# Gates first beside the state space, then values and conv gates by seven products on a normalised x, and the convolution's output projection by seven products through memory

## The chip, the cores and the metric

The kernel runs on one core of one Trainium2 chip. The metric is the device time of one execution in microseconds (us). A core has TensorE (PE, with its weight loads PEld), VectorE (DVE), ScalarE (ACT), GpSimd (POOL) and SyncE (SP), each with an instruction queue that runs in order, and DMA engines that move data between memory and the on-chip buffers.

## What is computed

A decoder block on x of 1024 positions by 1024 channels, in float32:

```
proj = rmsnorm(x) @ w_in + b_in      # 512 + 5 * 1024 columns
u, bg, cg, val, gs, gc = split(proj)
y = s5(u)                            # diagonal state space, 32 groups of 16 channels, 64 complex states
z = gelu(y)
y_a = (z @ w_glu_a) * sigmoid(z @ w_glu_b)
y_b = (bg * causal_conv3(cg * val)) @ w_conv_out
merged = sigmoid(gs) * y_a + sigmoid(gc) * y_b
h = x + merged @ w_out
h = h + relu(rmsnorm(h) @ w_ff1) ** 2 @ w_ff2      # 4096 columns
out = rmsnorm(h)
```

## The kernel before

All data lie with channels on the 128 partitions and positions along the row. A float32 operand is cut into a high part of a reduced type and the rest, so each product of a 128x128 weight block with 512 positions takes three matmuls: high by high, high by low and low by high (`products`, L135 to L137). The weights come as 1024x128 blocks of 512 KB: `w_load` (L87) loads one on SyncE's queue, `w_split` makes its high part wh on ScalarE (L95) and the rest wl on VectorE (L96).

The program is written out in one order, and each engine runs its rows of it in that order. Phase 0 normalises x and makes the first three blocks of u beside it. Then the loop over `order` runs 57 jobs: one block of u, eight each of val, cg, bg, gs and gc (48 matmuls each), the convolution's output (co, eight jobs of 48), and the eight of glu. Here the input projection uses x before its normalisation and multiplies each result by rstd on VectorE when it leaves PSUM. Behind it come the output projection (pw, `wo_half`), the second norm, four blocks of FF1 in plain form (pp), and then FF1 and FF2 in groups of seven products: `seven` computes a 2 by 2 block matrix product with seven half-size products instead of eight (84 matmuls for 96). In it P1 to P7 take operands B11, t1, B21, n2, B22, t3, t4 of the one side and sums of weight blocks (gs, cut into gh and gl) of the other. Its results c11, c12, c22, c21 are taken out of PSUM by `done`. The FF1 results go to memory and come back as the operands of FF2.

Beside the matmuls runs the state space. `ssm_params` computes its parameters on POOL; `cut_u` copies u into the layout U, 16 small pieces for each of four tiles, half on ScalarE and half on VectorE; `ssm_step` runs eight steps. Each makes the kernels Bk and Vk on POOL (`outer`) and the phases cs and sn, then transposes and small products on TensorE (pst, psk), psx, a rotation and scans on VectorE (xr, xi), the rotation back (yr, t) and psy; odd steps end with a gelu. These are generators. After each fourth group of three matmuls, `draw` gives them credit by the matmul time and the factor `BESIDE` of the current job, and an instruction sequence is put there. A negative yield postpones by modelled TensorE time, a positive one costs credit. `drain` runs all that is left at once; it stands before job gs 1. `ssm_z` then turns U into z.

In groups and rows below, a number behind a name is a buffer or job. The stages of the profiled execution by TensorE: phase 0 to 44.26 us, input projection with convolution output to 641.40, glu to 728.4, output projection to 816.9, plain FF1 to 862.9, groups to 1415, the last slab to the end.

## Time and profile before

| what | value |
|---|---|
| time, median of 3 runs | 1479.4 us (1478.95 to 1479.52) |
| the profiled execution | 1478.85 us, its span 1477.1 |
| TensorE busy | 1445.2 us, 98% |
| weight loads, VectorE | 1198.2 us, 967.4 us |
| ScalarE, POOL | 552.1 us, 223.6 us |
| moved | 161.10 MB, 109 GB/s in the mean |

The span is the time from the first to the last instruction of the profiled execution; its own time is somewhat longer. Busy times overlap between engines. TensorE's rows are pipelined, so one matmul's duration is longer than the distance between two starts, and the latter is its price.

### The profile page before, as it was taken

What the parts mean: (1) busy time and instruction counts of PE and PEld (TensorE: products, weight loads), DVE (VectorE), ACT (ScalarE), POOL (GpSimd) and SP (SyncE); (2) the same over time, 40 slices, a digit from 0 to 9 for tenths busy, and PEclk for the clock granted to TensorE, in tenths of its full rate; (3) what the DMA queues carried; (4) which work ended last, traced back from release to release, by engine and by line L of the source; (5) the groups of instructions that cost most, each with busy time, mean ns of one, the idle gap of its engine ahead of it and who ended that gap; (6) DMA issues with size and microseconds to landing.
All of it is one profiled execution on the core that took longest, in us unless ns stands there. A gap on an engine that the chain in (4) does not pass through costs nothing.

```text
span 1477.1 us, 17137 instructions
## 1 busy us (share of the span) xinstructions
PE 1445.2 (98%) x6563; PEld 1198.2 (81%) x6563; DVE 967.4 (65%) x1445; ACT 552.1 (37%) x803; POOL 223.6 (15%) x474
## 2 busy tenths in 40 slices
PE   9969999999999999999999999999999999999997
PEld 7858888888888888888888888888887878787897
DVE  6667468768767545446625887777775266758575
ACT  6541423132132227423313444334433443424354
POOL 5891220120120000000010012222222010000000
PEclk9989999999999999999999999999999999999998
DMA  5011101111111011114311234555559468445302
GB/s 216 29 43 41 46 29 55 33 42 58 35 37 57 29 58 43 57 43 163 139 54 58 86 129 160 180 175 180 183 199 347 163 163 253 178 153 218 115 29 86
DMA packets 48961, 161.10 MB, mean 109 GB/s; under 512 B 6256, under 2 KB 10736, under 8 KB 48880
## 3 DMA queue, kind: packets, MB, share of 16 engines
q1 hardware_dynamic: 35888, 117.02, 23.2%
q0 software_dynamic: 12992, 43.00, 8.6%
q8 instruction: 51, 0.84, 0.2%
q14 instruction: 30, 0.25, 0.1%
HBM read 117.00 MB, written 42.99 MB: 108 GB/s over the span
## 4 chain that ended last, share of the span: by engine, by line
PE 88%; POOL 5%; DVE 3%; issue 1%; DMA 1%; ACT 1%; SPq 0%; DVEq 0%; ACTq 0%; POOLq 0%
PE ps L135 9%; PE ps L137 9%; PE ps L136 9%; PE seed L1093 5%; PE seed L1095 5%; PE seed L1094 5%; PE pa L1095 3%; PE pa L1094 3%; PE pa L1093 3%; PE pe L1093 3%; PE pe L1095 3%; PE pe L1094 3%; PE pc L135 2%; PE pc L137 2%; PE pg L136 2%; PE pg L135 2%
## 5 line engine op out<-in xcount | busy, mean ns | idle before, releaser
L135 PE MATMUL ps<-xh,wh 128*128 128x512 f32 x656 | 258.9, 395 | 1.2 <-ACT wh L95 1.2
L137 PE MATMUL ps<-xh,wl 128*128 128x512 f32 x656 | 256.2, 391 | 0.5 <-DVE wl L96 0.5
L136 PE MATMUL ps<-xl,wh 128*128 128x512 f32 x656 | 255.7, 390 | 0.0
L135 PEld LDWEIGHTS ps<-xh,wh 128*128 128x128 f32 x656 | 123.5, 188 | 28.3 <-ACT wh L95 1.6
L137 PEld LDWEIGHTS ps<-xh,wl 128*128 128x128 f32 x656 | 123.4, 188 | 27.4 <-DVE wl L96 1.4
L136 PEld LDWEIGHTS ps<-xl,wh 128*128 128x128 f32 x656 | 123.6, 188 | 25.3
L96 DVE TENSOR_TENSOR wl<-wr,wh 128x1024 fp32r<-128x1024 f32 x57 | 70.1, 1230 | 58.2 <-ACT wh L95 58.0
L95 ACT ACTIVATE wh<-wr 128x1024 fp32r<-128x1024 f32 x57 | 59.6, 1047 | 55.4 <-PE pc L136 24.0
L1065 DVE TENSOR_TENSOR gl<-gs,gh 128x1024 fp32r<-128x1024 f32 x52 | 63.4, 1219 | 6.4 <-ACT gh L1061 6.4
L898 POOL DMA_DIRECT2D hd<-h x16 | 9.0, 561 | 384.1 <-ACT ssum L900 309.0
L1061 ACT ACTIVATE gh<-gs 128x1024 fp32r<-128x1024 f32 x52 | 54.8, 1054 | 20.1 <-DVE gs L1057 14.7
L135 PE MATMUL pc<-vh,wh 128*128 128x512 f32 x128 | 51.0, 399 | 0.0
L1065 DVE TENSOR_TENSOR gl<-rg,gh 128x1024 fp32r<-128x1024 f32 (+1 forms) x52 | 48.4, 951 | 3.4 <-ACT gh L1061 2.7
L137 PE MATMUL pc<-vh,wl 128*128 128x512 f32 x128 | 49.9, 390 | 0.0
L135 PE MATMUL pw<-mh,hwo 128*128 128x512 f32 x128 | 49.9, 390 | 0.0
L137 PE MATMUL pw<-mh,lwo 128*128 128x512 f32 x128 | 49.8, 389 | 0.0
L136 PE MATMUL pc<-vl,wh 128*128 128x512 f32 x128 | 49.8, 389 | 0.0
L136 PE MATMUL pw<-ml,hwo 128*128 128x512 f32 x128 | 49.8, 389 | 0.0
L135 PE MATMUL pg<-zh,wh 128*128 128x512 f32 x128 | 49.8, 389 | 0.0
L136 PE MATMUL pg<-zl,wh 128*128 128x512 f32 x128 | 49.8, 389 | 0.0
L137 PE MATMUL pg<-zh,wl 128*128 128x512 f32 x128 | 49.8, 389 | 0.0
L861 DVE TENSOR_TENSOR g<-ps,rstd 128x512 f32<-128x512 f32 x32 | 21.7, 687 | 41.5 <-PE ps L137 41.4
(531 smaller groups left out, 3603.2 us busy)
## 6 DMA issues: line engine op xcount, KB each, us to landing
rg<-in_w SPq DMA_DIRECT2D x52, 512.0 KB, 4.5
wr<-in_win SPq DMA_DIRECT2D x41, 512.0 KB, 3.5
wr<-in_wco SPq DMA_DIRECT2D x8, 512.0 KB, 3.4
wr<-in_wglu SPq DMA_DIRECT2D x8, 512.0 KB, 3.4
rwo<-in_wo SPq DMA_DIRECT2D x8, 512.0 KB, 6.7
h<-in_x_t SPq DMA_DIRECT2D x8, 512.0 KB, 7.4
hd<-h POOLq DMA_DIRECT2D x16, 256.0 KB, 2.3
rw<-in_w SPq DMA_DIRECT2D x8, 512.0 KB, 6.9
```

Source lines behind the costliest of these rows:

```text
L95: A.activation(hi, r, AF.Copy)
L96: V.tensor_sub(lo, r, hi.bitcast(F32))
L135: T.matmul(ps, wh[:, j, :], xh[:, cols], start=start and i == 0, stop=False)
L136: T.matmul(ps, wh[:, j, :], xl[:, cols], start=False, stop=False)
L137: T.matmul(ps, wl[:, j, :], xh[:, cols], start=False, stop=stop and i == n - 1)
L861: V.tensor_mul(t, ps[hh], rstd[:, HS[hh]])
L898: nc.gpsimd.dma_start(hd[i][:, c], h[i][:, c])
L1061: A.activation(hi[nm], src[nm], AF.Copy)
L1065: V.tensor_sub(lo[nm], src[nm], hi[nm].bitcast(F32))
L1093: T.matmul(p, wh[:, kb, :], xh, start=first and kb == 0, stop=False, skip_group_check=True)
L1094: T.matmul(p, wh[:, kb, :], xl, start=False, stop=False, skip_group_check=True)
L1095: T.matmul(p, wl[:, kb, :], xh, start=False, stop=kb == 3, skip_group_check=True)
```

## The change

The jobs of the loop are now u 3, seven gs, seven gc and eight bg: 23 blocks of 48 matmuls, beside which the state space runs. Their results are put through their sigmoid and go to memory (gd) on ScalarE's queue. Blocks 0 and 1 still use the unnormalised operand. While they run, x is read again, scaled by rstd on VectorE, written to memory (xnd) and cut into the operands xw of all later blocks (`normed_in`); the last blocks also make the sums t1, n2, t3, t4 of them (`sums_of`). `drain` stands before the last block. Then 13 groups of seven products run: four pairs of a val and a cg group, one of gs 7 with gc 7, and four of the convolution's output. The gated convolution of a pair is computed on VectorE and ScalarE in steps between the products (`conv_step`), its parts and sums go to memory (xcd) by POOL's queue and come back as operands xc by SyncE's (`XC_LOADS`). The output groups multiply by the gates read back as yb and write yd; glu reads gs, yd and z (zd) from memory. In the state space, half of the rotation back (t2, t3) moves from VectorE to POOL, and the waits in modelled time are changed. `seven` and `group_steps` serve all groups by one list, with the seeds made before the first.

```diff
-PREPARE = 20.0
+PREPARE = 38.0
...
-BESIDE = {"u": 0.4, "val": 0.62, "cg": 0.25, "bg": 0.38, "co": 0.28, "gs": 0.5, "gc": 0.5, "glu": 0.3}
+BESIDE = {"u": 0.4, "gs": 0.8, "gc": 0.8, "bg": 0.8}
...
-    order = [("u", 3)]
+    order = [("u", 3)] + [("gs", i) for i in range(7)] + [("gc", i) for i in range(7)] + [("bg", i) for i in range(8)]
...
-        yield 0.1
+        yield -3.0
...
-        yr, t2 = sh(f"yr{s}"), sh(f"t2{s}")
+        yr, t2, t3 = sh(f"yr{s}"), sh(f"t2{s}"), sh(f"t3{s}")
+        G.tensor_tensor(t2, xr, sn, op=ALU.mult)
+        G.tensor_tensor(t3, xi, cs, op=ALU.mult)
+        G.tensor_tensor(t3, t3, t2, op=ALU.add)
-        V.tensor_mul(t2, xr, sn)
-        V.tensor_mul(t, xi, cs)
-        V.tensor_add(t, t, t2)
-        yield 1.9
-        yield -4.0
+        yield -6.0
...
+            for q in range(4):
+                for j in range(CH):
+                    o, i = zv[32 * q:32 * q + 32, j, :], U[b][32 * j:32 * j + 32, q, :]
+                    if (q + j) % 2:
+                        A.activation(o, i, AF.Copy, scale=0.5)
+                    else:
+                        V.tensor_scalar(o, i, 0.5, None, op0=ALU.mult)
+                yield 0.8
+            nc.scalar.dma_start(zd[b], zt)
...
+    def split_out(nm, dst, t, lo=None):
+        hi = half(f"h{nm}", F32R)
+        A.activation(hi, t, AF.Copy)
+        nc.gpsimd.dma_start(dst("h"), hi.bitcast(F32))
+        def rest():
+            V.tensor_sub((t if lo is None else lo).bitcast(F32R), t, hi.bitcast(F32))
+            nc.gpsimd.dma_start(dst("l"), t if lo is None else lo)
+        later.append(rest)
...
+    def gated_conv(i):
+        v = val[i]
+        g = late.tile([P, S], F32, tag="l", name=f"bgt{i}")
+        nc.sync.dma_start(g, gd["bg", i])
+        o = og[i] = unit(f"og{i}")
+        A.activation(o, v, AF.Identity, scale=col(C_CW + 16 + i), bias=col(C_CB + i))
+        yield
+        for back in (1, 2):
+            V.scalar_tensor_tensor(
+                o[:, back:], v[:, :S - back], col(C_CW + 16 - 8 * back + i), o[:, back:], op0=ALU.mult, op1=ALU.add
+            )
+        yield
+        V.tensor_mul(o, o, g)
+    def to_xc(m, name, t, lo=None):
+        split_out(f"xc{name}{m}", lambda part: xcd[name, part][:, m, :], t, lo)
...
+    def conv_first(m):
+        yield from gated_conv(m)
+        f11, f12 = (og[m][:, c] for c in HS)
+        ta = og["a", m] = unit(f"xca{m}")
+        t1 = ta[:, HS[0]]
+        V.tensor_sub(t1, f11, f12)
+        to_xc(m, "B11", f11, half(f"lf11_{m}"))
+        to_xc(m, "t1", t1)
+        yield
+    def conv_second(m):
+        yield from gated_conv(m + 4)
+        (f11, f12), (f21, f22) = ([og[i][:, c] for c in HS] for i in (m, m + 4))
+        t3 = og["a", m][:, HS[1]]
+        n2, t4 = (unit(f"xcb{m}")[:, c] for c in HS)
+        V.tensor_sub(t3, f12, f22)
+        V.tensor_sub(n2, f11, t3)
+        yield
+        V.tensor_sub(t4, f21, n2)
+        to_xc(m, "B21", f21)
+        yield
+        to_xc(m, "n2", n2)
+        to_xc(m, "B22", f22)
+        yield
+        to_xc(m, "t3", t3)
+        to_xc(m, "t4", t4)
+        yield
...
+    def done_cg(m, quad, ps, less):
+        r, c = row_of(quad)
+        i = m + 4 * r
+        y, b = val[i][:, c], col(C_BIN + base["cg"] + i)
+        if less is not None:
+            t = half(f"cg{quad}_{m}")
+            V.tensor_sub(t, ps, less)
+            ps = t
+        V.scalar_tensor_tensor(y, ps, b, y, op0=ALU.add, op1=ALU.mult)
+        if quad == "c12":
+            conv.append(conv_first(m))
+        elif quad == "c21":
+            conv.append(conv_second(m))
...
+    def gate_load(g):
+        for o in (2 * g, 2 * g + 1):
+            yb[o] = unit(f"yb{o}")
+            nc.sync.dma_start(yb[o], gd["gc", o])
...
+    def done_co(g, quad, ps, less):
+        r, c = row_of(quad)
+        y = yb[2 * g + r]
+        if less is not None:
+            t = half(f"co{quad}_{g}")
+            V.tensor_sub(t, ps, less)
+            ps = t
+        V.tensor_mul(y[:, c], ps, y[:, c])
+        if quad in ("c21", "c12"):
+            nc.gpsimd.dma_start(yd[2 * g + r], y)
...
+    for m in range(4):
+        for k, f in (("val", done_val), ("cg", done_cg)):
+            add_group(from_rows(win[base[k] + m], win[base[k] + m + 4]), of_w, partial(f, m))
+    add_group(from_rows(win[base["gs"] + 7], win[base["gc"] + 7]), of_w, done_gate)
+    first_co = len(groups)
+    for g in range(4):
+        add_group(from_wco(2 * g, 2 * g + 1), of_c, partial(done_co, g))
+    first_f1 = len(groups)
+    for g in range(N_GROUP):
...
+    def normed_in(k, hh):
+        c = HS[hh]
+        t = half(f"xn{k}_{hh}")
+        nc.sync.dma_start(t, x_t[k * P:(k + 1) * P, c])
+        V.scalar_tensor_tensor(t, t, col(C_G1 + k), rstd[:, c], op0=ALU.mult, op1=ALU.mult)
+        nc.scalar.dma_start(xnd[k][:, c], t)
+        put(xw, f"B{1 + k // 4}{1 + hh}", k % 4, t)
...
+    def sums_of(kb):
+        (b11, b12), (b21, b22) = ([xn_raw[k][:, c] for c in HS] for k in (kb, kb + 4))
+        t = half(f"xt1_{kb}")
+        V.tensor_sub(t, b11, b12)
+        put(xw, "t1", kb, t)
+        V.tensor_sub(b12, b12, b22)
+        V.tensor_sub(b11, b11, b12)
+        put(xw, "n2", kb, b11)
+        put(xw, "t3", kb, b12)
+        V.tensor_sub(b21, b21, b11)
+        put(xw, "t4", kb, b21)
...
+    for n in range(n_main):
+        k, i = order[n]
+        clock["job"] = k
+        w_load(n + 2)
+        w_split(n + 1)
+        w_load(n + 3)
+        last = n == n_main - 1
+        ps = [bank(f"ps{n}_{j}") for j in range(2)]
+        if n < 2:
+            wh, wl = parts[n]
+            for kb, (xh, xl) in enumerate(xg):
+                for hh, c in enumerate(HS):
+                    T.matmul(ps[hh], wh[:, kb, :], xh[:, c], start=kb == 0, stop=False)
+                    T.matmul(ps[hh], wh[:, kb, :], xl[:, c], start=False, stop=False)
+                    T.matmul(ps[hh], wl[:, kb, :], xh[:, c], start=False, stop=kb == 7)
+            for kb in range(4 * n, 4 * n + 4):
+                for hh in range(2):
+                    normed_in(kb, hh)
+            if n == 1:
+                lows()
+        else:
+            if last:
+                group_load(0)
+                drain()
+                cvs.close()
+                late = ctx.enter_context(tc.tile_pool(name="late", bufs=12))
+            if n >= n_main - 3:
+                sums_of(n - (n_main - 3))
+            for hh in range(2):
+                xs = [operand(xw, f"B{1 + kb // 4}{1 + hh}", kb % 4) for kb in range(8)]
+                products(ps[hh], parts[n], range(8), xs, slice(0, HALF))
+        if n >= n_main - 4:
+            sums_load(n - (n_main - 4))
+        if k == "u":
+            evac_u(i, ps)
+            start(cut_u())
+            start(ssm_step(0))
+            continue
+        for hh in range(2):
+            t = half(f"e{n}_{hh}")
+            src = ps[hh]
+            if n == 1:
+                V.tensor_mul(t, src, rstd[:, HS[hh]])
+                src = t
+            A.activation(t, src, AF.Identity if k == "bg" else AF.Sigmoid, bias=col(C_BIN + base[k] + i))
+            nc.scalar.dma_start(gd[k, i][:, HS[hh]], t)
+    prep = group_steps(0, 0)
+    for _ in prep:
+        pass
...
+    XC_LOADS = {
+        0: [("B11", 0)], 1: [("B11", 1)], 2: [("t1", 0), ("t1", 1)], 3: [("B21", 0)], 4: [("n2", 0)],
+        5: [("B22", 0), ("B21", 1)], 6: [("t3", 0), ("n2", 1), ("B22", 1)], 7: [("t3", 1)], 8: [("t4", 0), ("t4", 1)],
+    }
...
+    for n in range(first_f1):
+        preps = [group_steps(n, 1), group_steps(n + 1, 0) if n + 1 < first_f1 else iter(())]
+        def after(i):
+            for prep in preps:
+                next(prep, None)
+            for _ in range(2 if n == first_co - 1 and i in (1, 2) else 1):
+                conv_step()
+            step_on()
+            for name, u in XC_LOADS.get(7 * (n - first_co + 1) + i, []):
+                xc_load(name, u)
+            if n >= first_co and i == 1:
+                gate_load(n - first_co)
+            if i == 6 and n + 2 < first_f1:
+                group_load(n + 2)
+            if n == first_f1 - 1:
+                if i == 2:
+                    glu_w[0] = raw_load(wglu[0], "glu0")
+                elif i == 4:
+                    glu_w[0] = cut(glu_w[0], "glu0", wtile)
+                if i in (3, 4, 5, 6):
+                    z_load(i - 3)
+                if i == 6:
+                    z_cut(0)
```

**TensorE, the end of the state space.** In before, psx of the last step and its psy have two blocks of the projection between them (ps is a block's PSUM, U the state space's input, yr and t the rotated states, ps_0_3872 to ps_1_3951 the two blocks):

```order
L539 MATMUL psxr_3841<-U_833,WT 128x256
L539 MATMUL psxi_3842<-U_833,WT 128x256
L135 MATMUL ps_0_3872<-xh_133,wh_3766 128x512
...
L137 MATMUL ps_1_3951<-xh_184,wl_3867 128x512
L573 MATMUL psy_4000<-U_833,Mk_204 128x256
L575 MATMUL psy_4000<-yr_3914,Vk_202 128x255
L575 MATMUL psy_4000<-t_3849,Vk_202 128x255
```

In the changed kernel the same place stands between block 21 (ps_1_2948) and block 22 (ps_0_3048); psy_3058 is of step 6, pst_3072, psxr_3087 and psy_3115 of step 7:

```order
L137 MATMUL ps_1_2948<-xhwB_934,wl_2804 128x512
L555 MATMUL psy_3058<-U_1067,Mk_203 128x256
...
L506 MATMUL pst_3072<-ident,Bk 128x128 x4
L509 MATMUL psk_3073<-Vk_202,Bk 32x128
L509 MATMUL psk_3073<-Vk_202,Bk 32x128 x3
L522 MATMUL psxr_3087<-U_1067,WT 128x256
...
L555 MATMUL psy_3115<-U_1067,Mk_204 128x256
L557 MATMUL psy_3115<-yr_3106,Vk_202 128x255
L557 MATMUL psy_3115<-t_3108,Vk_202 128x255
...
L135 MATMUL ps_0_3048<-xhwB_785,wh_2943 128x512
```

What moved: the 96 matmuls between psx and psy of the last step are gone, and its psy stands ahead of the last block.

**ScalarE, behind the first blocks.** In before, the cut of u (U) stands between two weight splits; v_1_0_839 is a result of the val block:

```order
L95 ACTIVATE wh_726<-wr_607 128x1024
L246 ACTIVATE U_746<-ut_609,pt 32x256 x8
L246 ACTIVATE U_763<-ut_612,pt 32x256 x8
L246 ACTIVATE U_804<-ut_615,pt 32x256 x8
L246 ACTIVATE U_833<-ut_723,pt 32x256 x2
L819 ACTIVATE v_1_0_839<-v_1_0_838,pt 128x512
L819 ACTIVATE v_1_1_843<-v_1_1_842,pt 128x512
L95 ACTIVATE wh_846<-wr_671 128x1024
```

In the changed kernel e is the gate of block 1 (e_1_956) and of block 2 (e_0_1076, e_1_1079), wh_960 the weights of block 3 and wh_1082 of block 4:

```order
L1136 DMA gsd_675<-e_1_956 128x512
L95 ACTIVATE wh_960<-wr_729 128x1024
L229 ACTIVATE U_980<-ut_609,pt 32x256 x8
L229 ACTIVATE U_1009<-ut_612,pt 32x256 x8
L229 ACTIVATE U_1038<-ut_615,pt 32x256 x8
L229 ACTIVATE U_1067<-ut_835,pt 32x256 x4
L1135 ACTIVATE e_0_1076<-ps_0_966,pt 128x512
L1136 DMA gsd_676<-e_0_1076 128x512
L1135 ACTIVATE e_1_1079<-ps_1_967,pt 128x512
L1136 DMA gsd_676<-e_1_1079 128x512
L95 ACTIVATE wh_1082<-wr_842 128x1024
```

What moved: the cut of u now stands two blocks later in the program, and two gates with their transfers stand between it and the next split.

**SyncE and VectorE, where the output groups begin.** Rows of SyncE in the changed kernel (xc are the operands of the convolution's output, rg weights of an output group, yb the gates gc that multiply the first output group's results); before has no such rows:

```order
L1154 DMA xlct_4677<-xct3l 128x1024
L1154 DMA xhct_4696<-xct4h 128x1024
L1154 DMA xlct_4698<-xct4l 128x1024
L1154 DMA xhct_4700<-xct4h 128x1024
L1154 DMA xlct_4702<-xct4l 128x1024
L1025 DMA yb_4704<-gcd_683 128x1024
L1025 DMA yb_4706<-gcd_684 128x1024
```

VectorE's rows at the same place (gs_10 and gl_10 belong to the weights of the second output group, gl_9 to the first's):

```order
L846 TENSOR_TENSOR gs_10_4724<-gs_10_4724,rg_0_4645 128x512
L1034 TENSOR_TENSOR yb_4704<-pa_4655,yb_4704 128x512
L857 TENSOR_TENSOR gl_9_4742<-rg_1_4421,gh_9_4722 128x512
L857 TENSOR_TENSOR gl_10_4744<-rg_0_4645,gh_10_4727 128x1024
L857 TENSOR_TENSOR gl_10_4761<-gs_10_4724,gh_10_4746 128x1024
```

What is new: yb stands behind all reads of xc on SyncE, and on VectorE two groups' weight splits stand behind the multiplication that needs it.

## Rows read from the trace of the kernel before

**Rows 1.** The page: GB/s moved in each of 40 equal slices of the span.

```profile
GB/s 216 29 43 41 46 29 55 33 42 58 35 37 57 29 58 43 57 43 163 139 54 58 86 129 160 180 175 180 183 199 347 163 163 253 178 153 218 115 29 86
```

**Rows 2.** Stretches: length, busy PE, PEld, DVE, ACT, POOL; granted clock, DMA share, GB/s.

```profile
44.26:641.40 597.14, 585.63 (x2609) 482.62 (x2608) 386.32 (x611) 205.03 (x292) 109.98 (x261) 0.99 0.14 44
...
92.85:109.20 16.35, 6.55 (x21) 3.94 (x20) 11.70 (x18) 5.12 (x10) 14.95 (x27) 0.59 0.10 31
149.40:641.40 492.00, 492.00 (x2210) 407.34 (x2209) 313.44 (x491) 161.13 (x232) 48.10 (x94) 1.00 0.14 44
...
863.20:1126.80 263.60, 263.60 (x1165) 218.23 (x1163) 195.55 (x270) 107.23 (x158) 63.55 (x118) 1.00 0.55 187
```

**Rows 3.** Waits of TensorE over the span: total us, times, longest.

```profile
PE pst L523 <- POOL Bk L484: 5.6, 2, 3.5
PE psk L526 <- POOL Vk L484: 4.2, 2, 2.3
...
PE ps L135 <- ACT wh L95: 1.2, 1, 1.2
```

**Rows 4.** Timeline of TensorE: start, duration, line; steady, then behind the POOL wait.

```profile
54.91 0.39 PE L137 MATMUL ps<-xh,wl 128*128 128x512 f32 x1
...
55.59 0.39 PE L137 MATMUL ps<-xh,wl 128*128 128x512 f32 x1
...
107.06 0.63 PE L136 MATMUL ps<-xl,wh 128*128 128x512 f32 x1
...
109.19 0.51 PE L135 MATMUL ps<-xh,wh 128*128 128x512 f32 x1
```

**Rows 5.** Timeline of ScalarE: the cut of u, and wh behind it.

```profile
56.20 3.04 ACT L246 ACTIVATE U<-ut,pt 32x256 f32<-32x256 f32 x4
...
77.14 1.04 ACT L95 ACTIVATE wh<-wr 128x1024 fp32r<-128x1024 f32 x1
```

**Rows 6.** Timeline of TensorE around a step's pst and psk, and around a psx.

```profile
150.44 0.60 PE L523 MATMUL pst<-ident,Bk 128*128 128x128 f32 x4
...
151.96 0.50 PE L135 MATMUL ps<-xh,wh 128*128 128x512 f32 x1
...
157.53 0.60 PE L539 MATMUL psxr<-U,WT 128*128 128x256 f32 x2
...
159.08 0.58 PE L135 MATMUL pc<-vh,wh 128*128 128x512 f32 x1
```

**Rows 7.** VectorE by line and shape, 44 to 641 us: busy us, mean ns.

```profile
L96 DVE TENSOR_TENSOR wl<-wr,wh 128x1024 fp32r<-128x1024 f32 x49 | 60.3, 1230 | 52.7 <-ACT wh L95 52.6
...
L839 DVE SCALAR_TENSOR_TENSOR cv<-vp,pt,cv 128x512 f32<-128x512 f32 x32 | 23.4, 753 | 0.6
...
L690 DVE TENSOR_SCALAR zt<-U 32x256 f32<-32x256 f32 x32 | 12.3, 385 | 0.4
...
L557 DVE TENSOR_TENSOR_SCAN xr<-sp_mags,xr 128x256 f32<-128x256 f32 x16 | 10.8, 673 | 0.0
...
L544 DVE TENSOR_TENSOR xr<-psxr,cs 128x512 f32<-128x512 f32 x8 | 5.5, 692 | 30.7 <-PE psxr L539 30.7
```

**Rows 8.** ScalarE by line and shape, the same stretch.

```profile
L95 ACT ACTIVATE wh<-wr 128x1024 fp32r<-128x1024 f32 x48 | 50.2, 1047 | 55.4 <-PE pc L136 24.0 <-issue 19.1 <-PE ps L136 12.3
...
L688 ACT ACTIVATE zt<-U 32x256 f32<-32x256 f32 x32 | 21.0, 656 | 0.4
...
L867 ACT ACTIVATE g<-g,pt 128x512 f32<-128x512 f32 x16 | 11.6, 724 | 61.0 <-DVE g L861 61.0
```

**Rows 9.** POOL by line and shape, the same stretch: its largest two-operand operation.

```profile
L294 POOL TENSOR_TENSOR bbt<-bc_raw,scratch 128x256 f32<-128x256 f32 x2 | 1.8, 924 | 0.0
```

**Rows 10.** The page's DMA issues (KB each, us to landing); one issue on SyncE's timeline.

```profile
wr<-in_win SPq DMA_DIRECT2D x41, 512.0 KB, 3.5
...
hd<-h POOLq DMA_DIRECT2D x16, 256.0 KB, 2.3
...
79.48 0.33 SPq L87 DMA_DIRECT2D wr<-in_win  x1
```

More of the change, by code (lines that the diff above doesn't have):

```diff
@@ new lines, in steps_of, with group_steps @@
+    def steps_of(gr, plan):
+        for step in plan:
+            for what in step.split():
+                gr["do"]["shl".index(what[0])](what[1])
+            yield
+    FIRST = ["", "", "s1 h0", "l0 h1", "l1"], ["s2 h2", "l2", "h3", "l3"]
+    SECOND = ["", "", "h3", "s1 l3", "h1", "l1"], ["s2 h0", "l0 h2", "l2"]
+    def group_steps(n, own):
+        gr = groups[n]
+        if "do" not in gr:
+            gr["do"] = w_parts(gr)
+        return steps_of(gr, (SECOND if gr["second"] else FIRST)[own])
@@ new lines, in chain, with seven @@
+    def chain(p, n, name, first):
+        gr = groups[n]
+        wh, wl = gr["w"][name]
+        for kb in range(4):
+            xh, xl = gr["ops"](X_OF[name], kb)
+            T.matmul(p, wh[:, kb, :], xh, start=first and kb == 0, stop=False, skip_group_check=True)
+            T.matmul(p, wh[:, kb, :], xl, start=False, stop=False, skip_group_check=True)
+            T.matmul(p, wl[:, kb, :], xh, start=False, stop=kb == 3, skip_group_check=True)
+    def seven(n, after, follows):
+        gr = groups[n]
+        done = gr["done"]
+        seed = seeds[n % 2]
+        pa, pe = bank(f"pa{n}"), bank(f"pe{n}")
+        chain(pa, n, "P1", True)
+        A.activation(seed, pa, AF.Copy, scale=-1.0)
+        after(0)
+        if follows:
+            last_product(n - 1)
+        after(1)
+        chain(pe, n, "P5", True)
+        if not gr["second"]:
+            sv = late.tile([P, S], F32, tag="l", name=f"sv{n}")
+            s5, v2 = (sv[:, c] for c in HS)
+        else:
+            s5, v2 = half(f"s5_{n}"), half(f"v2_{n}")
+        A.activation(s5, pe, AF.Copy)
+        after(2)
+        chain(pa, n, "P2", False)
+        done("c11", pa, None)
+        after(3)
+        chain(seed, n, "P6", False)
+        A.activation(v2, seed, AF.Copy)
+        after(4)
+        chain(pe, n, "P3", False)
+        done("c12", pe, v2)
+        after(5)
+        chain(seed, n, "P7", False)
+        done("c22", seed, s5)
+        after(6)
@@ L1089, in chain @@
-    def chain(p, g, name, first):
-        wh, wl = gw[g][name]
-        for kb in range(4):
-            xh, xl = operand(X_OF[name], kb) if g < N_GROUP else operand2(g, X_OF[name], kb)
-            T.matmul(p, wh[:, kb, :], xh, start=first and kb == 0, stop=False, skip_group_check=True)
-            T.matmul(p, wh[:, kb, :], xl, start=False, stop=False, skip_group_check=True)
-            T.matmul(p, wl[:, kb, :], xh, start=False, stop=kb == 3, skip_group_check=True)
     def sum_steps():
@@ L1147, in block_kernel @@
     plain(3, 1, some(2))
-    group_load(1)
+    group_load(first_f1 + 1)
     plain(0, 1, some(2))
-    seeds = [bank(f"seed{i}") for i in range(2)]
-    for s in seeds:
-        T.matmul(s, mhalf, operand("B11", 0)[0], start=True, stop=True)
     plain(1, 1, some(1))
```

571 lines of the change are left out of this document (248 added, 323 removed).

## The prediction, made before the changed kernel ran

> **What bounds the kernel now.** I read the page first, for how little most slices of the span move beside the best one, 347 GB/s [rows 1]. Then the time by stages: from 44.26 to 641.40 us (the input projection, the convolution's output, the state space between them) TensorE is busy 585.63 of 597.14 us, and from 149.40 on all of 492.00 [rows 2]. So TensorE is the bound, and what it loses there it loses early: its waits name POOL, late with Bk and Vk (5.6 + 4.2 us), and the weight split wh of ScalarE [rows 3]. TensorE's timeline prices a matmul of 128x512: three starts take 55.59 − 54.91 = 0.68, so 0.2267 us each. Behind the POOL wait five starts take 109.19 − 107.06 = 2.13, 0.43 each [rows 4]: the lower of the two clock levels (1.2 and 2.4 GHz), after TensorE had stood idle; the mean granted clock of 92.85 to 109.20 is 0.59 [rows 2]. Last I read what one operation of VectorE, ScalarE and POOL takes, and the landings of transfers.
>
> **The gains.** (1) Eight value, eight conv-gate and two gate blocks (18 x 48 = 864 matmuls) become nine groups of seven products (9 x 84 = 756); the convolution's output goes from 384 to four groups, 336. That is 156 fewer, x 0.2267 = **−35.4 us**, as long as TensorE stays the bound.
> (2) pst of the first step now stands 336 matmuls, 76 us, behind 44.26, so at 120 at the earliest; POOL's Vk was ready at 105 before. The waits of before go: the stretch 92.85 to 109.19 holds state-space matmuls that take 151.96 − 150.44 = 1.5 elsewhere [rows 6] (2.5 with their edges, my allowance) and six projection matmuls of 0.2267, 1.4; 16.3 − 3.9 = 12.4 are lost. With 2.3 at 76.7 to 80, where wh came late behind the U cut [rows 5], **−14.8**.
> Together −50.2.
>
> **The losses, in program order.** (a) Block 2 runs on a normalised x that VectorE makes beside blocks 0 and 1: 16 halves, each a scaling of 0.75 and a split of 0.69 [rows 7], 23 us, with a weight split (1.23) and two evacuations between them. It starts when x is reloaded, near 51, and ends near 76.5; TensorE ends block 1 at 66.0 and takes each half as it comes. Its block 2 ends at 81.7 where 76.9 was due: **+4.9** (2 to 8).
> (b) The U cut has only moved: on ScalarE (second piece of the order) 28 of its 32 pieces stand ahead of the evacuations of block 2 and of wh for block 4, where before 26 stood ahead of one wh. From one piece to the next takes 3.04/4 = 0.76 [rows 5], so 28 take 21.2: from 81.7 to 102.9. Two sigmoids (0.72) with an issue each (0.33, SyncE's price, since the trace has no issue on ScalarE) bring 105.0, wh (1.05) 106.0 [rows 8]. TensorE ended block 3 at 93.4: +12.7, 0.8 for wl behind wh, and 1.4 of half clock, the loss that six matmuls had after the POOL wait: **+14.9** (11 to 17). What waits meanwhile on VectorE and SyncE costs nothing, for TensorE waits anyway.
> (c) POOL now makes half of the back rotation, three operations of 128x512 a step, before the next outer products. The trace has 128x256 at 0.92 [rows 9]; 128x512 lies between 0.92 (size is free) and 1.85 (twice); I take 1.4, since POOL's smaller ones also grow less than by size. On four of the steps Vk is then ready about when TensorE asks: **+1.5** (0 to 8).
> (d) The drain. Before, 96 matmuls (22 us) lay between psx and psy of the last step (first piece of the order); now that step stands bare between blocks 21 and 22. TensorE's own work there is 9.4: psy, pst and psk, psx (159.08 − 157.53 = 1.55), psy [rows 6]. The chain, from the end of block 21: VectorE still has step 6's rotation and scans, a gelu, the sums for one operand pair, half of zt and the phases of step 7 ahead of cs: 22 operations of 128x512 (0.69), four scans (0.67), a weight split (1.23), eight zt (0.39), five of 0.44 and six of 0.35 to 0.49 [rows 7], 27 us, begun 11 us before the end of block 21 because they stand behind that block's weights. So cs comes at 16; WT stands behind it on ScalarE, 17.6; psx ends at 19.3; rotation 4.1, scans 2.7, POOL 3 x 1.4 = 4.2, the rest of psy 1.6: 31.9. Less 9.4 that is 22.5; if VectorE has no lag at all, 11 (from psx on nothing else can run). Nearest to the upper, as the rows stand in that order: 20, and 1.4 of half clock: **+21.4** (12 to 25).
> (e) From block 22 to the first group: the last gelus, 16 pieces of zt on two engines (ScalarE eight of 0.66, [rows 8]) and more sums stand ahead of the weights of group 0, which come at 51 after the start of the drain; TensorE is ready at 44.7. **+6** (3 to 9).
> (f) In a value group VectorE has 19.3 us of work by the rows of the order and these durations, in a conv-gate group 16.1, against 84 x 0.2267 = 19.04 on TensorE. FF1's groups run free at 195.55 of 263.60 us of VectorE [rows 2]; mean load 93% here. **+1.5** (0 to 8).
> (g) The results through memory. The gated convolution is written in 56 parts of 256 KB and read as 28 of 512 KB, 14.7 MB, within some 38 us from the first issue to the last product on them: 386 GB/s, more than the best slice (347). SyncE has all 28 ahead of yb of the first output group (third piece of the order); on VectorE the multiplication by yb stands ahead of two weight splits that TensorE needs. Alone such a read lands in 3.5 us, a write of 256 KB in 2.3 [rows 10]. By hand, with landings of 6: P4 of the last gate group waits 2.9 for its operand, and P6, P7, P4 of the next group 0.4, 1.6, 5.7 and 1.0: 11.6. If the reads land as quickly as alone, 2. I take **+9** (2 to 16).
> The Trainium skill, DMA: Bandwidth & Descriptors, table at the head, puts a core's memory near 358 GB/s and says that issuing from more engines doesn't raise it. By that rule 14.7 MB take 41 us and the term would be some 3 us larger; the trace's best, 347, agrees.
> (h) Glu opens with two z splits of 1.22 behind the last result on VectorE: **+2.2** (1 to 3).
> Losses: 4.9 + 14.9 + 1.5 + 21.4 + 6 + 1.5 + 9 + 2.2 = 61.4.
>
> **The sum.** 1478.85 (the profiled execution) − 50.2 + 61.4 = 1490.0; the median of the runs stands 0.5 above that execution: **1490.5 us**. Differences under 0.2% (3 us) can't be told from no change here. Losses under 47 make it faster.
>
> **Rivals.** *A, faster.* VectorE has no lag at the drain: (d) 11 + 1.4, (e) its low end 3, and the reads land quickly, (g) 3. Losses 4.9 + 14.9 + 1.5 + 12.4 + 3 + 1.5 + 3 + 2.2 = 43.4: **1472.5**. For it: over the stage VectorE was busy 386.32 of 597.14 [rows 2], so it has room in the mean. Against: its queue runs in order, and the operand sums were put into the same three blocks as the last steps. The lag decides: with (e) and (g) as in A it turns at a lag of some 4 us at cs.
> *B, a draw.* (d) near 16 with its clock, (g) 4, (e) 5: losses 50, **1479.4**.
> *C, the reads bind the output groups.* At 253 GB/s, the second best slice [rows 1], 14.7 MB take 58 us for 38: (g) becomes 20, **1501**, up to 1508 if the next weights are held up too. For it: the issue order on SyncE. Against it: the first ten reads have a whole gate group to land in.
>
> **How the numbers follow.** Forecast (losses 53 to 70) 0.52, A 0.25, B 0.12, C 0.11. The forecast's own range is 1482.5 to 1499. To leave out no more than 2 in 10 the range goes from 1468 (A with (b) at its low end) to 1508 (C). Faster 0.25, same 0.12, slower 0.52 + 0.11 = 0.63.
>
> **What would show it.** In the changed profile: TensorE waiting on wh for some 12 us after 93; no wait on Bk or Vk of the first step; ahead of psx and psy of the last step holes of 20 us together with a granted clock below 1 in that slice; a wait for gl before the first group; waits on the xc reads, or on gl behind yb, around the first output group; glu, wo, FF1 and FF2 as long as before within 1 us each. Holes of 12 us at the drain and no wait on reads would be A; waits of more than 8 us inside the value groups would mean that VectorE's count in (f) is too low, and the time above the forecast.

## The result, and the profile after

The changed kernel takes 1561.9 us (median of 4 runs, 1557.7 to 1565.0) against 1479.5: 1.0551 times the time before, 95% interval 1.0522 to 1.058. It is slower, as forecast, but by 82 us where 11 were forecast, and 54 above the highest time that the prediction gave a chance (1508). Its page: the span, busy time, and of 40 slices TensorE's busy tenths, its granted clock and GB/s (those of before are [rows 1]).

```profile
span 1560.8 us, 17513 instructions
...
PE 1439.8 (92%) x6407; PEld 1183.6 (76%) x6407; DVE 1026.0 (66%) x1459; ACT 621.7 (40%) x903; POOL 305.1 (20%) x562
...
PE   9757999999489997599999999999999999999997
...
PEclk9968999999689999799999999999999999999999
...
GB/s 205 209 61 90 72 67 96 68 84 146 27 148 140 184 181 251 363 201 197 207 174 104 58 85 137 176 179 186 178 182 233 241 188 200 257 97 254 94 50 100
```

TensorE fell from 98% to 92%. Three dips stand out, in slices 2 to 4, 11 to 12 and 16 to 17, and the granted clock falls in each. All that was lost was lost before glu, which begins at 725.7 us for 641.6; from there to the end both kernels take 835 us. The waits of TensorE between 40 and 740 us (total us, times, longest; [rows 3] before):

```profile
PE ps L136 <- DVE xlwB L736: 20.1, 4, 15.8
PE psxr L522 <- ACT WT L512: 13.6, 1, 13.6
PE ps L135 <- ACT wh L95: 11.2, 2, 10.8
PE psy L557 <- DVE yr L548: 9.9, 1, 9.9
PE psk L509 <- POOL Vk L467: 8.6, 5, 2.2
PE pa L887 <- DVE gl L857: 7.9, 1, 7.9
PE seed L885 <- DVE gatec L1016: 7.8, 1, 7.8
PE pa L885 <- ACT gh L853: 5.9, 1, 5.9
PE pa L885 <- DMA xhcB<-xcB21h: 4.9, 1, 4.9
...
PE ps L135 <- ACT xhwB L744: 4.6, 1, 4.6
```

These are the waits that the prediction named, at their places, and there is none on Bk or Vk of the first step; but the first row was to be a few us, and the rows on gl, gatec and xcB21h 9 together. The stretches show the rest (length, busy PE, PEld, DVE, ACT, POOL, granted clock, DMA share, GB/s; [rows 2] before):

```profile
66.00:100.10 34.10, 9.15 (x24) 5.22 (x25) 13.67 (x21) 4.90 (x9) 29.89 (x92) 0.66 0.39 136
...
450.85:603.17 152.32, 152.32 (x674) 126.13 (x672) 123.77 (x155) 70.75 (x97) 24.86 (x46) 1.00 0.47 166
...
620.00:640.00 20.00, 11.87 (x37) 9.00 (x38) 4.38 (x6) 3.36 (x5) 2.69 (x5) 0.76 1.02 403
640.00:660.00 20.00, 12.38 (x39) 9.16 (x37) 1.38 (x2) 3.60 (x5) 0.00 (x0) 0.76 0.96 338
```

From 450.85 to 603.17 the value and conv-gate groups run without a gap, eight lengths of 84 matmuls: 152.32 / 8 = 19.04 us. So the saving of matmuls is there in full. Block 2, from 66 on, is the largest hole, with POOL the one busy engine; around the first output group the DMA engines are full.

Behind most of the holes TensorE is slow for a while. Its timeline after the wait of block 4:

```profile
129.19 0.79 PE L135 MATMUL ps<-xhwB,wh 128*128 128x512 f32 x1 [10.82 <-ACT wh L95]
...
131.04 0.63 PE L135 MATMUL ps<-xhwB,wh 128*128 128x512 f32 x1
131.47 0.63 PE L136 MATMUL ps<-xlwB,wh 128*128 128x512 f32 x1
...
134.88 0.51 PE L135 MATMUL ps<-xhwB,wh 128*128 128x512 f32 x1
```

The starts lie 0.43 us apart, as in [rows 4], until 134.88. Starts further apart than 0.2267 us without a wait, summed over such stretches, cost 28 us in fourteen places between 44 and 740 us, nearly all of it at the lower granted clock; before there was one, of 1.4 us. Not every wait is followed by it. Inside block 2 the starts come at the full pace again behind a wait of 1.76 us:

```profile
70.17 0.50 PE L136 MATMUL ps<-xlwB,wh 128*128 128x512 f32 x1 [1.76 <-DVE xlwB L736]
70.52 0.40 PE L137 MATMUL ps<-xhwB,wl 128*128 128x512 f32 x1
70.75 0.40 PE L135 MATMUL ps<-xhwB,wh 128*128 128x512 f32 x1
```

### The profile page after: what moved, and what is told of

It is laid out like the page before. It is cut to its first block, busy times and chain, and to the rows that moved or that the text cites. A ratio compares the mean times of both kernels' runs of the same rounds, so it can differ in the third digit from the quotient of the medians.

```text
span 1560.8 us, 17513 instructions
## 1 busy us (share of the span) xinstructions
PE 1439.8 (92%) x6407; PEld 1183.6 (76%) x6407; DVE 1026.0 (66%) x1459; ACT 621.7 (40%) x903; POOL 305.1 (20%) x562
## 4 chain that ended last, share of the span: by engine, by line
PE 71%; DVE 8%; POOL 8%; DMA 5%; ACT 4%; issue 3%; SPq 0%; ACTq 0%; DVEq 0%; POOLq 0%
PE seed L885 6%; PE seed L887 6%; PE seed L886 6%; PE pa L887 4%; PE pa L885 4%; PE pa L886 4%; PE pe L885 4%; PE pe L887 4%; PE pe L886 4%; PE ps L135 2%; PE ps L137 2%; PE ps L136 2%; PE pw L135 2%; PE pw L137 2%; PE pw L136 2%
## 5 line engine op out<-in xcount | busy, mean ns | idle before, releaser
L136 PE MATMUL ps<-xlwB,wh 128*128 128x512 f32 x336 | 136.9, 407 | 20.1 <-DVE xlwB L736 20.1
L135 PE MATMUL ps<-xhwB,wh 128*128 128x512 f32 x336 | 140.3, 418 | 15.8 <-ACT wh L95 11.2
L137 PE MATMUL ps<-xhwB,wl 128*128 128x512 f32 x336 | 135.9, 405 | 0.6 <-DVE wl L96 0.5
L136 PEld LDWEIGHTS ps<-xlwB,wh 128*128 128x128 f32 x336 | 66.2, 197 | 35.9 <-DVE xlwB L736 22.4
L135 PEld LDWEIGHTS ps<-xhwB,wh 128*128 128x128 f32 x336 | 66.3, 197 | 33.1 <-ACT wh L95 12.0
L137 PEld LDWEIGHTS ps<-xhwB,wl 128*128 128x128 f32 x336 | 66.3, 197 | 16.0 <-DVE wl L96 1.7
L853 ACT ACTIVATE gh<-rg 128x1024 fp32r<-128x1024 f32 (+1 forms) x78 | 62.8, 838 | 0.4 <-ACT e L1135 0.4
L885 PE MATMUL seed<-xhft,gh 128*128 128x512 f32 x112 | 44.4, 397 | 3.3 <-DVE holdc L1487 3.3
L886 PE MATMUL seed<-xlft,gh 128*128 128x512 f32 x112 | 44.2, 395 | 0.0
L887 PE MATMUL seed<-xhft,gl 128*128 128x512 f32 x112 | 44.1, 394 | 0.0
```

The lines of the kernel that those rows point to most:

```text
L135: T.matmul(ps, wh[:, j, :], xh[:, cols], start=start and i == 0, stop=False)
L136: T.matmul(ps, wh[:, j, :], xl[:, cols], start=False, stop=False)
L137: T.matmul(ps, wl[:, j, :], xh[:, cols], start=False, stop=stop and i == n - 1)
L853: A.activation(hi[nm], src[nm], AF.Copy)
L885: T.matmul(p, wh[:, kb, :], xh, start=first and kb == 0, stop=False, skip_group_check=True)
L886: T.matmul(p, wh[:, kb, :], xl, start=False, stop=False, skip_group_check=True)
```

## The experiments

Each is set against the changed kernel's 1561.9 us. Those with one time are single executions; the changed kernel's own spread is 3 to 4 us either way, so differences below 5 us say nothing.

A part of that spread can be seen in the traces. In four of the runs (half of the reads, output weights in whole blocks, yb first, operands uncut) nothing is changed in the stage of the state space, and yet the first product of the output groups starts at 607.0, 607.7, 608.3 and 607.6 us, for 611.7 in the changed kernel: the same waits for Vk were followed by the lower clock on fewer of the steps. For these runs the gain at the place itself is given too, from that product to the first of glu, which takes 113.9 us in the changed kernel.

**Buffers apart.** Two tiles of POOL's parameter computation leave the pool of 34 units that also holds the operands xw:

```
-        scratch["t"] = unit("scratch")
+        scratch["t"] = spool.tile([P, S], F32, name="scratch")
-        u1 = unit("bbt")[:, :NQ * 16]...
+        u1 = spool.tile([P, NQ * 16], F32, name="bbt")...
```

> The changed kernel with two buffers of the parameter computation on POOL (scratch and bbt) taken out of the pool that also holds the operands of the normalised x. Theory 1: the 24 us hole at block 2 is a wait for these buffers, which POOL lets go at 87 and 94 us: the waits for xlwB and xhwB fall from 24.7 to under 8 us (the reload of x and VectorE's own pace are what is left), and the time falls by 18 to 27 us, to 1535 to 1544. Theory 2: the reload of x and VectorE's own work, as the prediction priced them, are slow, and the named buffers only come last: the waits stay over 18 us, the time within 5 us of 1561.9.

Measured: 1546.5 us, 15.4 less; TensorE's waits at block 2 fell from 24.7 to 8.1 us:

```profile
PE ps L136 <- DVE xlwB L736: 8.1, 5, 3.5
```

In the changed kernel VectorE and ScalarE stood for 14 and 20 us (start, duration, line; in brackets the idle time before it and what ended it):

```profile
87.33 0.88 DVE L736 TENSOR_TENSOR xlwB<-xn,xhwB 128x512 fp32r<-128x512 f32 x1 [13.99 <-POOL bbi L280]
...
94.65 0.63 ACT L744 ACTIVATE xhwB<-xn 128x512 fp32r<-128x512 f32 x1 [20.29 <-POOL sp_tl L280]
```

POOL does nothing for these rows; it only uses bbt and scratch to the end, and the tiles xlwB and xhwB were given their places. Theory 1 holds for two thirds of the hole, with a gain below the 18 to 27 expected. The 8 us left, with 5 of slow starts, are the reload of x and VectorE's pace, more than the prediction's 4.9: in this run VectorE idled 4.25 us for the second half of x and ended its last split at 83.8.

**Back rotation on VectorE.**

```
-        G.tensor_tensor(t2, xr, sn, op=ALU.mult)
-        G.tensor_tensor(t3, xi, cs, op=ALU.mult)
-        G.tensor_tensor(t3, t3, t2, op=ALU.add)
...
+        V.tensor_mul(t2, xr, sn)
+        V.tensor_mul(t3, xi, cs)
+        V.tensor_add(t3, t3, t2)
+        yield 1.9
```

> The changed kernel with the second half of the back rotation on VectorE again, as before the change. Theory 1: POOL's three operations of 1.5 us a step are what makes Vk late: the five waits of psk on Vk (8.6 us, and 6.8 of half clock behind them) go, and the drain loses 2.3 us; time down by 13 to 20, to 1542 to 1549. Theory 2: VectorE is full beside the state space, so the 2.1 us a step that come back to it delay psx, psy and the weights by as much: waits on VectorE of 8 us or more appear, time within 5 us of 1561.9.

Measured: 1539.8 us, 22.1 less. No psk waits for Vk any more, and the drain is shorter too, psxr 5.3 for 13.6 and psy 6.8 for 9.9 at the last step:

```profile
PE psy L558 <- DVE yr L545: 9.3, 2, 6.8
...
PE psxr L522 <- ACT WT L512: 5.3, 1, 5.3
```

Theory 1, with more than the 13 to 20 expected. In the changed kernel POOL's three operations take 4.86 us a step, and while they run VectorE's own three of the same rotation take 1.66 to 1.77 each instead of 0.69, on all eight steps. First the two engines in the changed kernel, then VectorE in this run (count, busy us, mean ns):

```profile
L543 POOL TENSOR_TENSOR t<-xr,sn 128x512 f32<-128x512 f32 x8 | 12.0, 1506 | 200.6 <-DVE xr L540 200.6
L546 DVE TENSOR_TENSOR yr<-xr,cs 128x512 f32<-128x512 f32 x8 | 13.7, 1715 | 0.0
```

```profile
L543 DVE TENSOR_TENSOR yr<-xr,cs 128x512 f32<-128x512 f32 x8 | 5.3, 665 | 0.0
L547 DVE TENSOR_TENSOR t<-xr,sn 128x512 f32<-128x512 f32 x8 | 5.5, 687 | 0.0
```

So the move took nothing off VectorE: its three operations beside POOL's take 5.1 us, all six alone 4.1. That is also why yr of the last step comes 3 us sooner here (3 x 1.0), as much as the wait for it fell (9.9 to 6.8). What the two engines share, the operands xr, xi, cs and sn or something behind them, no run separates. Why the phases of step 7 came earlier, which shortened the wait of psx, wasn't separated either.

**Steps earlier.** `-PREPARE = 38.0`, `+PREPARE = 20.0`.

> The changed kernel with the delay ahead of the first step at 20 as before the change; the steps move some 85 matmuls (19 us) ahead, and psx of the last step stands 38 matmuls ahead of the end of block 21. Theory 1: the drain is bare because the steps began late: the waits of psx and psy of the last step (23.5 us, some 4 us of half clock) fall under 10, time down by 14 to 22, to 1540 to 1548. Theory 2: VectorE is behind at the end whatever the start, since the sums for the operands stand in the same blocks: the two waits stay over 17 us, time down by less than 6.

Measured: 1551.4 us, 10.5 less: between the two. The wait for WT falls to 3.1, that for yr stays, for psx moved ahead of the end of block 21, the rotation behind it did not move ahead of the sums on VectorE:

```profile
PE psy L557 <- DVE yr L548: 10.0, 2, 9.5
...
PE psxr L522 <- ACT WT L512: 3.1, 1, 3.1
```

**U cut spread.**

```
-BESIDE = {"u": 0.4, "gs": 0.8, "gc": 0.8, "bg": 0.8}
+BESIDE = {"u": 0.4, "early": 0.3, "gs": 0.8, "gc": 0.8, "bg": 0.8}
-        clock["job"] = k
+        clock["job"] = "early" if 2 <= n < 5 else k
```

> The changed kernel with a credit factor of 0.3 in blocks 2 to 4, so that the U cut is spread over three blocks (12, 10 and 10 of 32 pieces on ScalarE). Theory 1: the queue of ScalarE alone makes wh of block 4 late: its wait (10.8 us, 3 of half clock) goes, time down by 11 to 14, to 1548 to 1551. Theory 2: block 4 waits for something behind it as well (the evacuations, wl): a wait of over 5 us stays in blocks 3 to 5.

Measured: 1546.8 us, 15.1 less; TensorE has no wait for wh of block 4 left. By the start of block 5 the run is 13.8 us ahead, within theory 1's 11 to 14. In the changed kernel ScalarE ran 28 pieces and the two gates first, just as the order had it:

```profile
104.70 21.11 ACT L229 ACTIVATE U<-ut,pt 32x256 f32<-32x256 f32 x28
...
128.08 1.06 ACT L95 ACTIVATE wh<-wr 128x1024 fp32r<-128x1024 f32 x1 [0.40 <-ACT e L1135]
```

**Half of the reads.**

```
-        for part in "hl":
-            t = unit(f"x{part}c{name}{u}", F32R)
+        t = unit(f"xhc{name}{u}", F32R)
...
-        xc[name, u] = ts
+        xc[name, u] = [t, t]
```

> The changed kernel in which the output groups read only the high part of each xc operand and use it for the low part too (the output of the convolution is computed from other numbers): 14 reads of 512 KB for 28, same places in the queue, all writes stay. Theory 1: the volume binds. The five waits between the last gate group and the second output group (7.8, 4.9, 0.8, 2.5, 7.9 us, and 9 of half clock, 33 together) fall under 10 together, time down by 22 to 33, to 1529 to 1540. Theory 2: the order binds: yb stands behind the other reads on SyncE and VectorE's multiplication ahead of the weight splits: the first waits go, that for gl stays over 5 us, time down by 8 to 18.

Measured: 1539.6 us, 22.3 less, and 21.2 less at the place. The five waits of 24 us became three of 8.9 (gatec 4.8, gl 3.1, sv 1.0); the DMA engines are still full for 20 us, but then done:

```profile
620.00:640.00 20.00, 15.87 (x65) 12.38 (x65) 6.28 (x9) 4.30 (x6) 0.00 (x0) 0.95 1.01 357
640.00:660.00 20.00, 20.00 (x87) 16.44 (x86) 12.39 (x17) 5.25 (x7) 1.62 (x3) 0.96 0.74 259
```

Theory 1, in the main.

**Output weights in whole blocks**, one issue for four (`nc.sync.dma_start(r, wco[o])`, the host's layout to match).

> The changed kernel with the convolution's output weights laid out so that one issue of 512 KB loads a block, for four of 128 KB with 1 KB to a row (as many bytes, 8 issues for 32). Theory 1: the volume binds, so the five waits of 24 us stay within 5 us, and the time within 6 of 1561.9. Theory 2: the many short issues on SyncE, which took 9.3 and 10.1 us for eight, hold up xc and yb: the waits for sv and gl (2.5, 7.9) go, time down by 10 to 18.

Measured: 1554.2 us, 7.7 less; at the place 4.7 less, within theory 1's 6. gl waits 2.1 for 7.9, but sv 4.3 for 2.5: partly moved.

**yb ahead of the last reads**, one step earlier on SyncE.

```
-            if n >= first_co and i == 1:
+            if n >= first_co and i == 0:
                 gate_load(n - first_co)
             for name, u in XC_LOADS.get(...):
```

> The changed kernel with the two reads of yb one step earlier, ahead of the last six reads of xc on SyncE (and of each output group one product earlier). If the order on SyncE is what holds up yb and the weight splits behind it on VectorE, the wait for gl (7.9 us) falls under 2 and the time by 6 to 10, to 1552 to 1556. If the volume binds, the wait only moves to the xc reads behind (t3, t4): the time stays within 4 of 1561.9.

Measured: 1554.7 us, 7.2 less, and 6.6 at the place. The wait for gl is gone, but xcB21h waits 7.0 for 4.9 and t3 and t4 come late (0.8, 1.5). Order is worth some 7 us here, volume some 22; the two aren't added, for both mend the same wait.

**Five operands uncut through memory**, cut behind the read.

> The changed kernel in which five of the seven xc operands go to memory and back as they are (only t1 and n2 as two parts) and are cut behind the read, as FF2 does: 18 reads of 512 KB for 28, 36 writes for 56; 10 cuts of 1.05 us on ScalarE and 1.22 on VectorE come between the products. Theory 1: the volume binds: the five waits fall from 24 to under 10 us, time down by 16 to 28, to 1534 to 1546. Theory 2: VectorE and ScalarE bind there, since their work ahead of the products grows by 12 and 10 us: waits on VectorE of over 12 us stay, time down by less than 8.

Measured: 1549.7 us, 12.2 less (11.5 at the place), between the two. The first waits went; new ones of 14.7 us in six are for the cuts (the longest ScalarE's xhcB 7.3 and VectorE's xlcB 3.4). With 18 reads the DMA engines are full from 600 to 640 too (362 and 343 GB/s); ScalarE stood 5.8 us for a transfer ahead of the cut that TensorE waited longest for.

**All mends at once**, with x reloaded by halves of the row and the steps at full credit.

> All mends at once: POOL's buffers apart and x read by halves of the row with the next weights behind it, rotation back on VectorE, the U cut over three blocks, the steps at full credit from 24 us on with the waits of before, xc unsplit, the output weights whole. If the losses are the five mechanisms and stand for themselves, TensorE's bare work (44.3 + 2196 x 0.2267 + 49 + 835 = 1426) and some 10 to 25 us of rest remain: 1437 to 1452, faster than before by 27 to 42. If VectorE is the bound behind them, its waits fill the state-space stage and the groups: over 1465.

Measured: 1480.0 us, 1.0007 times the time before (0.9997 to 1.0017): no difference from before, and 28 us over the upper end of the first theory. The time lies where the second theory put it (over 1465), but its sign isn't there: of the waits ahead of glu VectorE ends 13 us and ScalarE 19, and the value groups run without one. The six mends that were also run on their own gave 15 + 22 + 10 + 15 + 12 + 8 = 82 us, and together the gain is 82. That they add up isn't shown by it, for this kernel has two mends more (x by halves, full credit), and some of the single gains are the spread told above. 32 us of short waits were left, and some 10 of lower clock behind them; my 10 to 25 had no clock in it.

**Four more mends** (gates 7 on POOL's queue, B11 in two parts, weights of block 3 and group 0 cut earlier, 2 us more ahead of psx of the first step).

> The kernel with all mends, and four more: the two gates of the last gate group go to memory on POOL's queue (on ScalarE the issue waited over 4 us and the cuts of xc behind it), B11 of xc as two parts again, the weights of block 3 cut ahead of block 1's gates and those of group 0 ahead of block 22's, and 2 us more between the phases and psx of the first step. If each of the waits left in the kernel with all mends has the cause that its trace names, the waits of wh (4.4), WT (4.2), gh (3.3) and of xc (13.7 in six) fall from 26 to some 10 us with half of the clock loss behind them: 1452 to 1466, faster than before by 13 to 26. If the transfers between the last gate group and the output groups bind whatever stands on the queues, only the first three go: 1466 to 1474.

Measured: 1481.8 us (1.0007 to 1.0027): a miss for both theories. The wait for WT fell from 4.2 to 0.6, but two of the others came back next door (wh of block 4 5.9 for that of block 3 4.4; xhwt 3.3 for gh 3.3), and around the output groups the DMA engines stay full:

```profile
540.00:560.00 20.00, 12.42 (x42) 7.92 (x40) 6.50 (x8) 4.44 (x6) 3.00 (x6) 0.83 1.02 382
560.00:580.00 20.00, 11.95 (x32) 8.32 (x33) 10.14 (x11) 10.34 (x12) 0.26 (x1) 0.76 0.90 358
```

**Plain convolution output.** On the kernel with all mends, 48 matmuls more, but one third of the reads:

```
-    for g in range(4):
-        add_group(from_wco(2 * g, 2 * g + 1), of_c, partial(done_co, g))
...
+    for o in range(8):
+        for hh, c in enumerate(HS):
+            p = bank(f"pc{o}_{hh}")
+            products(p, cw[o], CO_ORDER, [vg[k] for k in CO_ORDER], c)
+            V.tensor_mul(yb[o][:, c], p, yb[o][:, c])
+        nc.gpsimd.dma_start(yd[o], yb[o])
```

> The kernel with all mends, in which the convolution's output is computed in plain form again (384 matmuls for 336, +10.9 us): only the gated convolution itself goes through memory, six reads of 512 KB for 18, and its last two blocks stay on the chip. Also the two gates of the last gate group on POOL's queue, and the U cut from block 2 to 5 with the weights of block 3 ahead of block 1's gates. If the volume of the reads is what binds around the output groups, the waits there (13.7 us in seven, and some 6 of half clock) fall under 5 together: 1465 to 1474, faster than before. If VectorE's and ScalarE's work in the last gate group binds, waits for cuts of over 8 us stay: 1476 or more.

Measured: 1473.6 us, 0.9965 times the time before (0.9951 to 0.9979): 0.35% faster than before. The waits between the last gate group and the first output blocks are 2.9 and four under 0.9, 5.6 in all, a little over the 5 expected, with 3.4 us at the lower clock (538.8 to 542.2). The reads lie in the 20 us ahead of this stretch (276 GB/s); the stretch itself moves 92. Of the 6 us gained on the kernel with all mends 4 lie ahead of the first group, where the U cut and the weights of block 3 were moved; at the place the plain form little more than pays for its 10.9 us of matmuls:

```profile
540.00:560.00 20.00, 16.92 (x64) 11.89 (x63) 8.86 (x9) 8.58 (x10) 1.64 (x3) 0.94 0.26 92
```

**Holes filled** with matmuls of no use into a spare bank, 170 in all: 46 ahead of block 4, 58 ahead of psx and 42 ahead of psy of the last step, 24 ahead of the first group.

```
+            if n == 4:
+                fill(46, "f4")
+        if s == 7:
+            fill(58, "fx")
+        if n == 0:
+            fill(24, "f0")
```

> The changed kernel with matmuls into a spare bank put into four of its holes, about as many as fill them: 46 ahead of block 4 (wait 10.8 us), 58 ahead of psx and 42 ahead of psy of the last step (13.6, 9.9), 24 ahead of the first group (5.9). Nothing else is changed, and what TensorE waits for comes when it came. If the slow matmuls behind each hole are the clock, which a busy TensorE keeps, the four holes give back what the records show behind them (3.0 + 1.7 + 1.4 + 3.3 = 9.4 us, less what the filling overruns): 7 to 9 us faster than the changed kernel's 1561.9, 1553 to 1555, and matmuls start every 0.23 us at once behind them. If they are slow for another reason (operands that come one by one, weights late), the slow stretches stay and the time is 1561 or more.

Measured: 1552.3 us (median of 4, 1550.8 to 1555.7), 1.0502 (1.0484 to 1.052) for 1.0551 (1.0522 to 1.058). 9.6 us less by the medians, with more work on TensorE. Behind the filled hole of block 4 the matmuls start at the full pace at once:

```profile
129.38 0.50 PE L135 MATMUL ps<-xhwB,wh 128*128 128x512 f32 x1 [0.73 <-ACT wh L95]
129.72 0.40 PE L136 MATMUL ps<-xlwB,wh 128*128 128x512 f32 x1
```

and the same stretch at both clocks, first of the changed kernel (129.19 to 134.88), then of this one, with 12 and 22 matmul records:

```profile
129.19:134.88 5.69, 5.65 (x12) 3.97 (x13) 2.98 (x5) 4.71 (x7) 0.00 (x0) 0.50 0.13 49
```

```profile
129.38:135.07 5.69, 5.16 (x22) 3.98 (x23) 2.96 (x5) 4.71 (x7) 0.00 (x0) 1.00 0.13 50
```

So the slow starts are the lower clock level, and filling the hole before them kept the higher one. The size agrees with the 9.4 of the records only by luck. By the two traces some 6 us came from the four holes, since at the full pace TensorE met new short waits behind two of them (wl 0.5; gl 0.5 and a seed 1.0); 4.4 came between block 5 and the end of block 21, where nothing was filled. There the waits for Vk are as long in both kernels, but this time the lower level follows two of them and not four. The first one, in the changed kernel and in this one:

```profile
195.52 0.84 PE L509 MATMUL psk<-Vk,Bk 128*32 128x128 f32 x6 [1.83 <-POOL Vk L467]
...
197.54 0.63 PE L135 MATMUL ps<-xhwB,wh 128*128 128x512 f32 x1
```

```profile
193.54 0.84 PE L509 MATMUL psk<-Vk,Bk 128*32 128x128 f32 x6 [1.85 <-POOL Vk L467]
...
195.58 0.40 PE L137 MATMUL ps<-xhwB,wl 128*128 128x512 f32 x1
```

## Why the prediction was wrong

The gains stand: 35.4 us of matmuls at 19.04 us a group, and the first step waits for nothing. The losses, from the changed kernel's trace (waits, and the slow starts behind them):

| term | forecast | waits | slow starts | together |
|---|---|---|---|---|
| (a) operands of block 2 | 4.9 | 25.2 | 4.9 | 30.1 |
| (b) U cut ahead of wh | 14.9 | 10.8 | 3.0 | 13.9 |
| (c) Vk late behind POOL's rotation | 1.5 | 8.6 | 6.8 | 15.4 |
| (d) the drain | 21.4 | 23.5 | 3.8 | 27.3 |
| (e) weights of the first group | 6 | 5.9 | 3.3 | 9.2 |
| (f) VectorE inside the groups | 1.5 | 0 | 0 | 0 |
| (g) results through memory | 9 | 23.9 | 9.2 | 33.1 |
| (h) glu's start | 2.2 | 1.8 | 0.8 | 2.6 |
| sum | 61.4 | 99.7 | 31.8 | 131.6 |

131.6 − 50.2 = 81.4, of the 83.7 by which the span grew (1560.8 − 1477.1).

(a) **The step that failed first**: "ends near 76.5". VectorE's own 23 us were counted, but not where the operands are put. Their tiles took the places of POOL's bbt and scratch, which POOL uses until 87 and 94 us, so two engines stood still behind a third that made nothing for them. Giving POOL its own tiles took 15 us off. The remaining third was a size: x is reloaded through six small buffers, and its second half stands behind a load of weights on SyncE. With POOL out of the way VectorE ended at 83.8, not 76.5.

(g) The mechanism was right and the size wrong: 33 for 9, beyond rival C's 20. The volume was counted (14.7 MB over 38 us), but the hand count then took landings of 6 us. The 28 reads landed 3.8 to 16.4 us after their issue, 10.2 in the median. By the program operands can only be read when the last gate group has let go of the old ones, product by product, and each is wanted some 19 us, one group, later; the writes of the last pair, 3.7 MB, and the weights fall into the same time. From 620 to 660 the core moved 403 and 338 GB/s and TensorE had 37 and 39 records. VectorE's gate result waited too, for a small buffer whose write was caught behind the reads:

```profile
621.66 0.75 DVE L1016 SCALAR_TENSOR_TENSOR gatec<-seed,pt,sv 128x512 f32<-128x512 f32 x1 [6.62 <-DMA xcB22h<-hxcB]
...
660.33 0.69 DVE L1034 TENSOR_TENSOR yb<-pa,yb 128x512 f32<-128x512 f32 x1 [10.63 <-DMA yb<-gcd]
```

Halving the reads gave 22 us, putting yb first 7: the volume is the main cause, the order on the queue a part. At the best rate seen, 403, the reads alone take 14.7 / 0.403 = 36.5 us, nearly all of the 38 that the prediction gave them; with the 3.7 MB of writes it is 45.7, before any weights. The Trainium skill, DMA: Bandwidth & Descriptors, table at the head, has 358 GB/s for a core's memory, which the prediction set beside its sum; the 403 measured here is 13% above it. The Trainium skill, Perfetto Trace Analysis, Roofline, says that a core alone may pass it by about a fifth, and the 403 agrees with that.

**The clock** was the term that was left nearly out. The prediction charged 1.4 us twice; slow starts cost 31.8 us in all, nearly all of it at the lower level (the 0.8 at glu's start isn't). Here they came behind each of the ten waits of 2.5 us and more. Behind shorter ones they came in part: four waits of 1.8 to 2.2 us for Vk were followed by them here, and only two of the same four in the kernel with filled holes. Behind the four holes that were filled the records show 9.4 us, of which filling gave some 6 back.

(c) POOL's operation was priced nearly right (1.51 to 1.73 for 1.4), and Vk is late on four steps, as many as the prediction named, by 1.8 to 2.9 us in five waits. What was left out is the clock, here nearly as much again, and that VectorE's own half of the rotation slows beside POOL's (5.1 us a step for 2.0).

(d) held in its mechanism: psx of the last step began 403.07 − 384.89 = 18.2 us after block 21 for 17.6 forecast, and yr came 10.9 us after the last psx for 11, though what ended that wait was VectorE's slowed half (5.1 us) and not POOL's 4.2:

```profile
403.07 1.22 PE L522 MATMUL psxr<-U,WT 128*128 128x256 f32 x2 [13.61 <-ACT WT L512]
...
406.64 1.06 PE L555 MATMUL psy<-U,Mk 128*128 128x256 f32 x2
417.57 1.22 PE L557 MATMUL psy<-yr,Vk 128*128 128x255 f32 x2 [9.87 <-DVE yr L548]
```

Only psx and psy themselves ran at the lower level. (b), (e) and (h) came within some 3 us, and (b) fell away when the cut was spread. In (b) the sum puts the end of block 3 at 93.4, where 81.7 and 48 starts of 0.2267 make 92.6. (f) was too careful: the groups run free at a VectorE load of 123.77 of 152.32 us.

Rival C named the right place. No rival had buffers, and none had the clock as a price on the waits. That the direction came out right is the part of the prediction that holds; the terms that made the size are the waits of (a) and (g) and the clock, 81 us together (25.2 + 23.9 + 31.8) for 16.7 in the sum (4.9 + 9 + 2.8).

What stays open: why moving the rotation to VectorE also shortened the wait of psx, and what of the 32 us of short waits in the kernel with all mends could go together; mending four of them one by one moved most of them. It also stays open what decides whether the lower clock follows a wait of 1.6 to 2.2 us.

## What to carry to other kernels

Before a new operand is priced, look whose place in the pool it takes and when the last reader lets go: a wait can come from an engine that has no part in the work. Where results go through memory to save on-chip space, the time for the reads runs from the release of the old operands to the use of the new, and the bytes over that time, writes and weights included, have to fit the best rate of the trace. And a hole on TensorE costs its length and the slow starts behind it: here a third more on average (99.7 and 31.8), though not behind each short one. Before work is moved to an idle engine, look what runs beside it at that moment: POOL's half of the rotation made VectorE's half 2.5 times as long.
